# Branch hints ahead of the tests of a mixture-of-experts kernel: three engines are told which way each test goes

## The chip, the cores and the metric

The kernel runs on one core of one Trainium2 chip. The metric is the device time of one execution in microseconds (us). Before the change it was 739.19 us, the median of three runs (738.68 to 739.32). Five engines of the core work side by side, each with a program of its own: TensorE (PE in the profile; PEld is its weight load), VectorE (DVE), ScalarE (ACT), GpSimd (POOL) and SyncE (SP), which here issues the transfers from memory. They wait for each other through semaphores. A letter q behind an engine's name (PEldq, SPq) means its sequencer: waits, branches, register instructions and DMA issues, in which the engine itself stands idle.

## The reference, cut to what matters

Two layers, 256 tokens of width 1024. Each layer is a token mixer (attention, a state-space model and latent attention) and then a mixture of experts, which alone is touched here:

```python
def hier_moe(x, w_rg, b_rg, w_re, b_re, w_gate, w_up, w_down):
    ...                       # gate[n, g, e]: two experts of one group per token, the rest 0
    for g in range(N_EXPERT_GROUPS):           # 4 groups of 8 experts, hidden width 256
        h = jax.nn.silu(jnp.einsum('nd,edf->enf', xt, w_gate[g])) * jnp.einsum('nd,edf->enf', xt, w_up[g])
        h = h * gate[:, g].T[:, :, None].astype(h.dtype)
        y = y + jnp.einsum('enf,efd->nd', h, w_down[g])
```

All 32 experts' weights are read in every layer, 3 MB for each expert. Which tokens go to which expert is known only at run time, and so is the number of tokens that an expert gets.

## The kernel before

The function `moe(l, tab, rt)` takes the experts of a layer in nine blocks, in an order that the table `ORDER` fixes: seven blocks of four experts (here called quads) and two of two experts in layer 0, and the same numbers in layer 1. A block gathers the tokens of its experts by a one-hot matmul (`gather`, L1236), multiplies with the gate and up weights in two halves of the contraction (`gate_up`, L1442), forms the gated hidden values (`hidden`: silu on ACT, L1347, a product on DVE, L1348), transposes them on PE (`hidden_t`), multiplies with the down weights (`down`, L1458), splits the result into a high part (ACT, L1360) and a low part (DVE, L1361), and adds it to the tokens by two more matmuls and an add (`combine`, L1251 to L1253). The add of one block stands behind the gate and up matmuls of the next.

In a quad an expert has 32 places. Should an expert of it have more tokens than that, a second pass over the quad's weights is needed (`second`): the first half of it stands inside a test at L1559 and the other inside a test at L1589, both on the same register `more`, which L1554 loads on every engine. An expert with more than 64 tokens needs extra units: `unit_chain` (L1424) holds seven of them as nested tests, each of which reloads one expert's weights and works 128 places. It stands after the block `UNIT_AT`, the fourth block of layer 0 and the sixth of layer 1, and tests a number `nu` that L1606 loads. With these inputs no unit runs in layer 0 and one runs in layer 1, and one quad in layer 1, the one behind the unit, needs the second pass. All other tests skip their body. A body that is skipped is jumped over on every engine, and in its place an engine runs a few semaphore increments (EVENT_SEMAPHORE at L1424, L1559, L1589), for which others wait.

Weights come through one DMA queue that SP issues (`pump`, L247) in a fixed order into pages of 1 MB, of which there are 25. A page is refilled when the block that read it is done (`done`), and an issue also waits until one of eight earlier transfers has landed. SP goes through the same tests, in its own order. The order of instructions on each engine is the scheduler's of the framework: it moved the test at L1559 behind both halves of `gate_up` in nearly all quads.

## Time and profile before

| what | value |
|---|---|
| median of three runs | 739.19 us |
| the profiled execution | 737.13 us, of which 735.4 us are the span of the program |
| PE busy | 631.6 us, 86% of the span |
| DVE, ACT, POOL busy | 51%, 34%, 15% |
| transfers | 232.90 MB, 317 GB/s over the span |
| first mixture of experts | about 165 to 372 us |
| second mixture of experts | about 505 to 720 us |

The profile cuts the span in 40 slices of 18.4 us. In slices of steady expert work the DMA engines move 400 to 417 GB/s and are busy in nine tenths or more of the time; in the mixers they move far less. The transfers named "instruction" in the profile are the engines' own program code: 53 packets on queue q8 and 34 on queue q14. The 16 KB packets of q8 come as the PE's program goes on, which the prediction uses.

### The profile page before, as it was taken

What the parts mean: (1) busy time and instruction counts of PE and PEld (TensorE: products, weight loads), DVE (VectorE), ACT (ScalarE), POOL (GpSimd) and SP (SyncE); (2) the same over time, 40 slices, a digit from 0 to 9 for tenths busy, and PEclk for the clock granted to TensorE, in tenths of its full rate; (3) what the DMA queues carried; (4) which work ended last, traced back from release to release, by engine and by line L of the source; (5) the groups of instructions that cost most, each with busy time, mean ns of one, the idle gap of its engine ahead of it and who ended that gap; (6) DMA issues with size and microseconds to landing.
All of it is one profiled execution on the core that took longest, in us unless ns stands there. A gap on an engine that the chain in (4) does not pass through costs nothing. (4 is left out here: it accounts for less than half of the span.)

```text
span 735.4 us, 12004 instructions
## 1 busy us (share of the span) xinstructions
PE 631.6 (86%) x4370; PEld 386.3 (53%) x4370; DVE 373.7 (51%) x899; ACT 253.2 (34%) x578; POOL 107.5 (15%) x135
## 2 busy tenths in 40 slices
PE   7997989889799498598799899989899987769994
PEld 6584877744245334336268677775444434324442
DVE  3899977532334117824279878752423324322424
ACT  3647873421012014524074397352111211001113
POOL 1202001000000021521051754510000000000001
PEclk9999999999899799889999999989999999979998
DMA  8920375896999899999994715895999999998992
GB/s 304 419 108 0 117 289 215 331 389 231 413 406 416 280 405 411 412 415 407 398 417 183 286 59 172 302 362 194 333 416 406 392 410 413 416 366 301 410 382 83
DMA packets 57207, 232.90 MB, mean 317 GB/s; under 512 B 6048, under 2 KB 8480, under 8 KB 48160
## 3 DMA queue, kind: packets, MB, share of 16 engines
q1 hardware_dynamic: 57120, 231.75, 81.5%
q8 instruction: 53, 0.87, 0.5%
q14 instruction: 34, 0.28, 0.1%
HBM read 233.82 MB, written 1.05 MB: 319 GB/s over the span
## 5 line engine op out<-in xcount | busy, mean ns | idle before, releaser
L1442 PE MATMUL gu<-pg,xe 128*32 128x512 f32 (+1 forms) x1024 | 147.9, 618 | 12.4 <-DMA pg<-in_w_up_dram 7.1
L1458 PE MATMUL yp<-pg,scr 128*32 128x512 f32 (+2 forms) x560 | 79.4, 639 | 25.9 <-DVEq L1589 11.5
L1442 PEld LDWEIGHTS gu<-pg,xe 128*32 128x32 f32 (+1 forms) x1024 | 48.1, 117 | 96.7 <-issue 91.0
L1236 PE MATMUL gp<-oh,xn 128*128 128x128 f32 (+1 forms) x416 | 71.2, 325 | 4.0 <-DVE oh L1221 2.0
L1236 PEld LDWEIGHTS gp<-oh,xn 128*128 128x128 f32 x416 | 61.4, 197 | 18.6 <-issue 10.6
L1458 PEld LDWEIGHTS yp<-pg,scr 128*32 128x32 f32 (+1 forms) x560 | 22.1, 120 | 73.0 <-issue 58.2
L1361 DVE TENSOR_TENSOR y<-yp,y 128x512 fp32r<-128x512 f32 (+1 forms) x39 | 26.3, 677 | 65.8 <-ACT y L1360 65.8
L1348 DVE SCALAR_TENSOR_TENSOR scr<-gu,gs,scr 128x256 f32<-128x256 f32 x19 | 9.1, 481 | 97.1 <-ACT scr L1347 97.1
L1228 POOL TENSOR_TENSOR pgt<-oh,gate 128x256 f32<-128x256 f32 (+1 forms) x13 | 10.2, 783 | 316.5 <-PE slp L372 304.6
L1253 DVE TENSOR_TENSOR x<-cp,x 128x512 f32<-128x512 f32 x76 | 48.9, 685 | 14.2 <-PE cp L1252 14.2
L1360 ACT CAST y<-yp 128x512 fp32r<-128x512 f32 (+1 forms) x39 | 22.3, 575 | 88.1 <-PE yp L1458 86.6
L359 DVE TENSOR_SCALAR xe<-gp,vec 128x128 f32<-128x128 f32 (+1 forms) x52 | 20.8, 400 | 52.0 <-PE gp L1236 52.0
L355 ACT ACTIVATE xe<-gp,vec 128x128 f32<-128x128 f32 (+1 forms) x52 | 21.3, 409 | 73.3 <-PE gp L1236 73.2
L1347 ACT ACTIVATE scr<-gu 128x256 f32<-128x256 f32 x19 | 7.3, 384 | 102.3 <-PEq L1559 52.3
L1251 PE MATMUL cp<-y,sm 128*128 128x512 f32 x76 | 34.0, 455 | 0.3 <-PEq L1559 0.2
L1252 PE MATMUL cp<-y,sm 128*128 128x512 f32 x76 | 30.4, 409 | 1.5 <-DVE y L1361 1.5
L1058 DVE SCALAR_TENSOR_TENSOR x<-op,rg,x 128x512 f32<-128x512 f32 x24 | 17.9, 749 | 16.8 <-PE op L681 11.9
L1341 ACT ACTIVATE scr<-slp 128x256 f32<-128x256 f32 x20 | 7.8, 388 | 42.2 <-SPq L1424 28.8
L1251 PEld LDWEIGHTS cp<-y,sm 128*128 128x128 f32 x76 | 14.5, 192 | 10.4 <-issue 8.2
L372 PE MATMUL hp<-cst,scr 128*128 128x128 f32 x40 | 9.3, 314 | 12.2 <-DVE scr L1348 11.1
L372 PE MATMUL slp<-cst,pgt 128*128 128x128 f32 x36 | 8.3, 314 | 11.2 <-DVEq L1424 5.9
L1252 PEld LDWEIGHTS cp<-y,sm 128*128 128x128 f32 x76 | 14.3, 193 | 5.5 <-DVE y L1361 3.8
(454 smaller groups left out, 1209.2 us busy)
## 6 DMA issues: line engine op xcount, KB each, us to landing
pg<-in_w_gate_dram SPq DMA_DIRECT2D x128, 512.0 KB, 10.1
pg<-in_w_up_dram SPq DMA_DIRECT2D x128, 512.0 KB, 10.4
pg<-in_w_down_dram SPq DMA_DIRECT2D x56, 1024.0 KB, 11.8
pg<-in_w_o_dram SPq DMA_DIRECT2D x8, 1024.0 KB, 18.0
pg<-in_w_down_dram SPq DMA_DIRECT2D x12, 512.0 KB, 10.4
pg<-in_w_qk_dram SPq DMA_DIRECT2D x4, 1024.0 KB, 14.9
pg<-in_w_nat_dram SPq DMA_DIRECT2D x4, 960.0 KB, 12.8
wgu<-in_w_gate_dram SPq DMA_DIRECT2D x4, 512.0 KB
```

The costliest lines, as they stand in the source:

```text
L355: S.copy(dst, src) if scale is None else S.activation(dst, src, AF.Copy, scale=scale)
L359: e.tensor_scalar(dst, src, scale, None, op0=OP.mult)
L372: PE.transpose(dst, src, ident[:src.shape[0], :src.shape[0]])
L1058: V.scalar_tensor_tensor(xh, p, rg[:, g, tt:tt + 1], xh, op0=OP.mult, op1=OP.add)
L1236: PE.matmul(p[:, :w], xn[:, tt, k, :], P[:, tt].rearrange("p e c -> p (e c)"), start=(tt == 0), stop=(tt == 1))
L1251: PE.matmul(p, Sm[:, 128 * tt:128 * tt + 128], yh[:, c], start=True, stop=False)
L1252: PE.matmul(p, Sm[:, 128 * tt:128 * tt + 128], yl[:, c], start=False, stop=True)
L1253: V.tensor_tensor(x[:, tt, c], p, x[:, tt, c], OP.add)
L1360: S.copy(yh[:, c], yp)
L1361: V.tensor_tensor(yl[:, c], yp, yh[:, c].bitcast(F32), OP.subtract)
L1442: PE.matmul(gu[m * s:m * s + m, :].rearrange("p (a f) -> p a f", a=2), xs(k, s), page(l, "gu", e, hf)[:, :, k % 4, :], start=(k == 0), sto ...
L1458: PE.matmul(yp[m * s:m * s + m, :], hT[:, j, m * s:m * s + m], page(l, "dn", e)[:, j, c], start=(j == 0), stop=(j == 1), tile_position=(0, ...
```

## The change

Ahead of a test, three engines (PE, ACT, DVE) get two instructions: one that forms the condition in a register (REGISTER_ALU) and one that names a coming branch and, by that register, its direction (BRANCH_PREFETCH_HINT). SP and POOL get none. Nothing else is computed, and no semaphore is added. The place of the pair is fixed by `tc.issue_after`: behind the last matmul, activation or vector instruction that the dictionary `at` holds for the engine. The number `nu` is loaded some instructions earlier than before.

```diff
+            at = {}
+            def hint(label, cond):
+                for name, ins in at.items():
+                    with tc.issue_after(ins.ins):
+                        tc.mark_branch_hint_location(label, hint=cond, engines=[getattr(mybir.EngineType, name)])
...
             def hidden(gu, gs):
-                S.activation(sl, gu[:, 0:256], AF.Silu)
-                V.scalar_tensor_tensor(hh, gu[:, 256:512], gs, sl, op0=OP.mult, op1=OP.mult)
+                at["Activation"] = S.activation(sl, gu[:, 0:256], AF.Silu)
+                at["DVE"] = V.scalar_tensor_tensor(hh, gu[:, 256:512], gs, sl, op0=OP.mult, op1=OP.mult)
...
             def unit_chain(nu, u):
-                with tc.If(nu > u):
+                with tc.If(nu > u, label=f"unit{l}_{u}"):
                     if u:
                         unit_load(u)
                     unit(u)
                     if u + 1 < MAXU:
+                        hint(f"unit{l}_{u + 1}", nu > u + 1)
+                    if u + 1 < MAXU:
                         unit_chain(nu, u + 1)
...
+                    if k in (1, 7):
+                        at["PE"] = ins
...
                         if b > 0:
-                            with tc.If(more > 0):
+                            hint(tag + "a", more > 0)
+                            with tc.If(more > 0, label=tag + "a"):
                                 second(blk, w, 0)
...
                     hh = hidden(gu, gs)
+                    if quad:
+                        hint(tag + "b", more > 0)
...
                     if b == UNIT_AT[l]:
+                        n = 2 * MAXU
+                        nu = nc.values_load(uw["ui"][0:1, n:n + 1], min_val=0, max_val=MAXU)
+                        hint(f"unit{l}_0", nu > 0)
                         combine(pend)
                         pend = None
-                        n = 2 * MAXU
-                        unit_chain(nc.values_load(uw["ui"][0:1, n:n + 1], min_val=0, max_val=MAXU), 0)
+                        unit_chain(nu, 0)
```

On PE, at the test of the extra units in layer 0, before: the last of the matmuls of `combine` (cp), the load of `nu` (from the tile ui), the test, and the first matmul of a unit's body (gpu).

```order
L1251 MATMUL cp<-y,sm 128x512
L1252 MATMUL cp<-y,sm 128x512
L1606 TENSOR_LOAD ui
L1424 COMPARE_AND_BRANCH
L1398 MATMUL gpu<-xn,Pu 128x512 x4
```

The same place now, from the last matmul of `down` (yp) on:

```order
L1470 MATMUL yp_2257<-pg,scr 64x512 x4
L1619 TENSOR_LOAD ui
L1336 REGISTER_ALU
L1710 BRANCH_PREFETCH_HINT
L1251 MATMUL cp<-y,sm 128x512
L1252 MATMUL cp<-y,sm 128x512
```

The load and the hint went ahead of the eight matmuls of `combine`, behind which the test (now L1432) follows directly. Inside each of the first six units of the chain stands a pair too, that of the next unit's test:

```order
L1251 MATMUL cp<-y,sm 128x512 x2
L1336 REGISTER_ALU
L1710 BRANCH_PREFETCH_HINT
L1252 MATMUL cp<-y,sm 128x512 x2
L1432 COMPARE_AND_BRANCH
```

There two matmuls stand between the hint and the test.

On PE, at a quad (the third block of layer 0), before: the gate and up matmuls (gu) of both halves, the load of the flag (qi), the test, and the body's first matmuls (gpa).

```order
L372 MATMUL slp<-cst,pgt 128x128 x2
L1442 MATMUL gu<-pg,xe 32x512 x32
L1554 TENSOR_LOAD qi
L1559 COMPARE_AND_BRANCH
L1474 MATMUL gpa<-scr,xn 128x128 x16
```

And now:

```order
L372 MATMUL slp<-cst,pgt 128x128 x2
L1452 MATMUL gu<-pg,xe 32x512 x16
L1566 TENSOR_LOAD qi
L1336 REGISTER_ALU
L1710 BRANCH_PREFETCH_HINT
L1452 MATMUL gu<-pg,xe 32x512 x16
L1336 REGISTER_ALU
L1710 BRANCH_PREFETCH_HINT
L1572 COMPARE_AND_BRANCH
```

The load of the flag and the first pair went into the middle of the matmuls; the second pair, which belongs to the quad's later test, stands directly before the first test. In the whole program PE has 39 such pairs, ACT 40 and DVE 28; those inside units that do not run are jumped over.

## Rows read from the trace of the kernel before

**Rows 1.** Stretches: us, busy time by engine, granted clock, DMA share, GB/s

```profile
262.00:300.00 38.00, 33.79 (x234) 14.88 (x226) 22.71 (x68) 12.78 (x25) 9.06 (x12) 1.00 1.02 414
400.00:505.00 105.00, 96.55 (x602) 73.96 (x602) 74.03 (x190) 57.58 (x137) 45.87 (x52) 0.95 0.65 229
505.00:622.00 117.00, 105.08 (x686) 52.43 (x683) 38.21 (x80) 21.59 (x56) 3.95 (x5) 0.99 0.94 372
664.00:672.00 8.00, 8.00 (x72) 5.08 (x76) 2.89 (x6) 0.75 (x3) 0.00 (x0) 1.00 0.90 263
```

**Rows 2.** What SP's DMA issues waited for, 300 to 385 us: total, times, longest

```profile
SPq L247 <- DMA pg<-in_w_down_dram: 20.7, 15, 2.2
...
SPq L247 <- PEq L1559: 1.3, 1, 1.3
```

**Rows 3.** PE in order of time, 345 to 386 us: start, length, what [idle before]

```profile
357.74 1.91 PE L1442 MATMUL gu<-pg,xe 128*32 128x512 f32 x12 [1.59 <-DMA pg<-in_w_up_dram]
...
368.37 1.90 PE L1458 MATMUL yp<-pg,scr 128*32 128x512 f32 x10 [0.22 <-DMA pg<-in_w_down_dram]
```

**Rows 4.** PE in order of time, 236 to 262 us

```profile
236.74 0.51 PE L1251 MATMUL cp<-y,sm 128*128 128x512 f32 x1
...
238.81 0.39 PE L1252 MATMUL cp<-y,sm 128*128 128x512 f32 x1
244.48 0.66 PE L372 MATMUL slp<-cst,pgt 128*128 128x128 f32 x2 [5.29 <-PEq L1424]
249.48 9.11 PE L1442 MATMUL gu<-pg,xe 128*32 128x512 f32 x64 [4.34 <-issue]
```

**Rows 5.** Line L1424, 200 to 300 us: count, ns min/median/max, first and last start

```profile
L1424 SPq EVENT_SEMAPHORE  x9: 17/17/17, 244.3 to 248.8; - x9
...
L1424 PEldq COMPARE_BRANCH  x1: 5411/5411/5411, 238.7 to 238.7; - x1
```

**Rows 6.** DMA queue q8, 239.5 to 244.2 us: packets, MB, share of 16 engines

```profile
q8 instruction: 1, 0.02, 1.6%
```

**Rows 7.** DMA queue q8, 244.2 to 249.5 us

```profile
q8 instruction: 1, 0.02, 1.1%
```

**Rows 8.** DMA queue q8, 400 to 505 us

```profile
q8 instruction: 4, 0.07, 0.2%
```

**Rows 9.** SP in order of time, 250 to 262 us

```profile
252.85 7.14 SPq L247 DMA_DIRECT2D pg<-in_w_down_dram  x4
```

**Rows 10.** What SP's DMA issues waited for, 236 to 262 us

```profile
SPq L247 <- PEq L1559: 5.0, 1, 5.0
```

**Rows 11.** Stretches of layer 0 behind the test of the units, columns as in rows 1

```profile
252.40:255.30 2.90, 2.90 (x27) 1.99 (x23) 0.00 (x0) 0.00 (x0) 0.00 (x0) 0.84 1.04 410
255.30:258.80 3.50, 3.30 (x32) 1.76 (x24) 0.00 (x0) 0.07 (x1) 0.00 (x0) 1.00 0.98 284
```

**Rows 12.** Line L1424, 600 to 700 us

```profile
L1424 SPq EVENT_SEMAPHORE  x9: 17/17/17, 657.7 to 662.8; - x9
...
L1424 PEldq COMPARE_BRANCH  x3: 70/176/6028, 624.1 to 653.1; - x3
```

**Rows 13.** PE in order of time, 644 to 664.5 us

```profile
654.18 9.71 PE L1442 MATMUL gu<-pg,xe 128*32 128x512 f32 x64
```

**Rows 14.** Waits of all engines, 645 to 672 us

```profile
ACT scr L1341 <- SPq L1424: 17.2, 1, 17.2
DVE scr L1486 <- ACT scr L1341: 9.3, 1, 9.3
```

**Rows 15.** Line L1589, the whole span

```profile
L1589 PEldq COMPARE_BRANCH  x15: 78/318/1681, 182.8 to 717.5; - x15
L1589 ACTq COMPARE_BRANCH  x15: 38/45/50, 183.2 to 717.9; - x15
```

**Rows 16.** Line L1606, the whole span

```profile
L1606 SPq FUSED_REGOPS  x2: 147/156/165, 202.3 to 663.0; - x2
```

**Rows 17.** Line L1554, 655 to 664 us

```profile
L1554 PEldq TENSOR_LOAD <-qi x1: 304/304/304, 661.1 to 661.1; - x1
```

## The prediction

> **What bounds the kernel now.** I read the stretches first, then who the DMA queue waits for, then PE around each test. In the steady part of the experts the DMA engines are busy all the time and move 414 GB/s, while PE is busy in 89% (33.79 of 38 us) [rows 1]. There SP's issues wait for SP's own earlier transfers, 20.7 us of it for down weights alone between 300 and 385 us, and for PE only 1.3 us [rows 2]. PE waits for weights to the end of layer 0: 1.59 us for the last gate and up pages, 0.22 us in the middle of the last down [rows 3]. So the end of an expert stage is set by the moment when its last page lands, and PE time matters only where it holds up an issue of SP or where the queue isn't full: at the start of layer 1's experts (372 GB/s [rows 1]), and at the tests of the extra units.

> The reader should next see the test of the units in layer 0. PE stands idle for 5.29 us, does two small matmuls and stands idle for another 4.34 us, for which the trace finds no waker [rows 4]. The first of the two gaps is PE's branch over all seven units, which takes 5.41 us [rows 5]. In each of the two gaps one 16 KB packet of program code comes on q8 [rows 6, 7]. I take both for fetches of code: the landing place of the jump, and the piece of program behind it. How long a piece is follows from the mixer, which has no branch: 602 matmuls and 602 loads went by with 4 packets [rows 1, 8]. With 4 to 5 fetches in 1204 instructions an estimate is 240 to 300 instructions each. Between the landing and the second gap PE issues the two slp matmuls with their loads, one load of gu, and the waits before them, about ten instructions. The landing thus stands about ten instructions before the end of a piece.

> **The change part by part.**

> 1. *The hint of the units' test on PE, layer 0.* It now stands ahead of eight combine matmuls, and the branch comes behind them. Those matmuls end with the row at 238.81 [rows 4]; eight at about 0.25 us each (the first started at 236.7, the last at 238.8) put the hint some 2 us before the branch. If the fetch starts at the hint and is as long as before, PE goes on 2 us earlier; if the hint is too late to do anything, 0. Both are kept.

> 2. *The moved code on PE, layer 0.* Ahead of the landing PE gets ten pairs: one for the second block, two for the third, one for the units, and six inside the units. These are 20 instructions, and a piece ends at a fixed count. A landing that stood ten before the end of a piece then stands about ten behind it, with some 230 to go. So the second gap, 4.34 us, goes whatever the hint does. This rests on no instruction having been added or taken away elsewhere ahead of it, which the order of PE shows, and on the count of ten, which may be wrong by a few; if it were over 20, the gap would stay.

> 3. *What these are worth.* Without the second gap alone PE starts its 64 gate and up matmuls at about 245.1 and not at 249.48, and is done 9.1 us later, at 254.2 instead of 258.6; with the 2 us of the hint at 252.2. The hidden values need ACT's copy of the places, which waits for SP's last semaphore at 248.8 [rows 5], so ACT is not later than PE. The next work of PE waits for pages. The time is then worth what it gives the DMA queue. SP issued a down page at 252.85 and the next only after a wait of 5.0 us for PE's test at L1559 [rows 9, 10]. For that the queue ran low: 284 GB/s between 255.3 and 258.8, after 410 [rows 11]. The loss is 3.5 us x (1 - 284/410) = 1.1 us. With PE done by 254.2, SP doesn't wait at all and the loss is gone: **-1.1 us**. If only the hint works and the gap stays, PE is done at 256.6 and about 60% of it is gone, -0.65 us. If neither works, 0. Behind it the queue is full up to the end of layer 0 [rows 1, 2], and PE waits for its pages there [rows 3], so these 1.1 us are not lost again; the mixer and layer 1 follow as a chain and shift with them.

> 4. *The units of layer 1.* The jump out after one unit costs PE 6.03 us [rows 12], and the hint stands two matmuls ahead of it, under 1 us. I count nothing: PE did 64 gate and up matmuls until 663.9 [rows 13], and for the second pass behind them it needs DVE (L1486), which waited 9.3 us for ACT, which waited 17.2 us for SP's semaphores at L1424 [rows 14]. SP gives these out from 657.7 to 662.8 [rows 12], each when a transfer of its own has landed, and SP has no hint. An earlier PE would wait for DVE.

> 5. *The quads.* PE's branch takes 318 ns in the middle and 1.68 us at worst [rows 15]; the three slow ones I leave in, since PE's queue or the pages cover them. ACT's branch takes 45 ns [rows 15]: there is nothing to win on ACT, whose first hint stands directly before its test, and little on DVE.

> 6. *The price of the pairs.* Some 28 are run on PE. No row shows one. From below stands a branch of ACT, 45 ns [rows 15], from above SP's register instruction, 156 ns [rows 16], so a pair takes 0.09 to 0.31 us, and 28 of them 2.5 to 8.7 us if all were in the way. I take 0: PE's loads of the flag take 0.30 us and stand in the middle of its matmuls, which ran from 654.18 to 663.9 without an idle row [rows 13, 17], because the sequencer is ahead of the engine. On ACT and DVE the pair follows an instruction behind which the engine waits for PE. Where the cover is gone, at the start of layer 1, the four quads' pairs would add 0.7 to 2.5 us.

> The sum for the profiled execution is 735.4 - 1.1 = 734.3 us of span, and with the 1.73 us around it 736.0 against 737.13. That execution lies 2.06 us below the median, so I carry the difference over: 739.19 - 1.1 = **738.1 us**.

> **The rivals.**

> *Nothing happens* (the hint comes too late, and the landing stays at the end of a piece): 739.2. For it: with quads, too, the pair often stands next to the test. Against it: the 20 added instructions shift the landing without the hint's help.

> *More than the dip is won.* When SP's queue stays full, its later wait for PE of 1.3 us [rows 2] may go as well, and PE is earlier by 6 us, so any such wait in layer 0 shrinks: -1.1 - 1.3 = -2.4, 736.8. Against it: PE then runs on the pages' time again within a block.

> *Slower: a hint takes the place of the code that comes next.* If an engine fetches one piece ahead, and a hint makes it fetch the piece of the branch target in its stead, the engine meets the end of its present piece without the next one. The price is one such gap, 4.34 us [rows 4]. With a full queue a single gap is covered by pages in store; it decides from the first that falls where the queue is not full: among the four quads at the start of layer 1, or in the second pass behind the unit, where PE runs without an idle moment and the queue moves 263 GB/s [rows 1]. One: 739.2 + 4.3 - 1.1 = 742.4; two: 746.7. For it: 13 of 14 quads jump, and pairs of two tests stand together, the later one ahead of the earlier test. Against it: the target of a quad's test lies 140 to 170 instructions on, mostly in the piece that comes next anyway.

> [...]

> **How the numbers follow.** My forecast gets 0.50, nothing 0.18, more 0.17, slower 0.15. A measurement of this kernel tells 0.2%, 1.5 us, from no change. The forecast and "nothing" lie within that; a part of the forecast (0.08) may turn out over 1.5 us, and 0.03 of it slower, by uncovered pairs. So faster is 0.25, the same 0.57, slower 0.18. The range goes from 736.2, a little under the rival that wins more, to 742.3, one uncovered gap; the likeliest case's own range, with the bounds of parts 1, 2 and 6, is 737.0 to 739.9.

> **What would show it.** In layer 0 the profile should show one idle gap of PE of 3 to 5 us at the units' test and none behind the slp matmuls; SP's wait of 5.0 us for PE at L1572 gone; about 410 GB/s in place of 284 right behind; the rest of the trace earlier by about 1 us. In layer 1 ACT should still wait for SP's semaphores until some 661 to 663 us. I am wrong if PE gets new gaps without a waker at quads (slower), if the second gap stays, or if the 1.1 us won at 260 us are not there any more at 372.

## The result, and the profile after

The changed kernel is slower: 762.80 us (median of 4 runs, 757.71 to 765.28) against 739.26 us, a ratio of 1.0292 with a 95% interval of 1.0254 to 1.0329. The forecast was 738.1 us, its range ended at 742.3. The profiled execution took 757.71 us, of which 755.8 us are the span.

PE in order of time, in layer 0, answers to [rows 4] (start, length, what, [idle before <- who ended it]):

```profile
210.62 1.06 PE L1470 MATMUL yp<-pg,scr 128*32 128x512 f32 x7 [1.37 <-DVEq L1604]
216.65 5.39 PE L1470 MATMUL yp<-pg,scr 128*32 128x512 f32 x25 [4.97 <-issue]
...
251.51 0.66 PE L372 MATMUL slp<-cst,pgt 128*128 128x128 f32 x2 [4.97 <-DVEq L1432]
252.10 8.61 PE L1452 MATMUL gu<-pg,xe 128*32 128x512 f32 x64
...
262.85 2.77 PE L1470 MATMUL yp<-pg,scr 128*32 128x512 f32 x23 [0.51 <-ACTq L1604]
268.70 2.60 PE L1470 MATMUL yp<-pg,scr 128*32 128x512 f32 x9 [3.07 <-issue]
```

The second gap of [rows 4], 4.34 us, is gone, as forecast. The first is about as long as before, but now DVE ends it: DVE's own jump over the units, from its branch to its landing, takes 4.8 us (246.6 to 251.4 us) where it took 1.0 us (239.6 to 240.6). New are gaps in the middle of the down matmuls of a quad, for which the trace finds no waker. Over the whole program the page has 13.6 us of such idle time at this line:

```profile
L1470 PE MATMUL yp<-pg,scr 128*32 128x512 f32 (+2 forms) x560 | 84.1, 662 | 39.3 <-issue 13.6
```

In the kernel before, the same group (L1458) is idle for 25.9 us, most of it in waits for DVE, ACT and pages, and none of its gaps over 0.5 us is without a waker. The first new gap has a packet of program code in it (DMA queues, 211.7 to 216.7 us), like the gaps of [rows 6, 7]:

```profile
q8 instruction: 1, 0.02, 1.3%
```

The branch over the units of layer 0, L1432 (count, ns min/median/max, first and last start), which answers to [rows 5]:

```profile
L1432 PEldq COMPARE_BRANCH  x1: 5200/5200/5200, 245.6 to 245.6; - x1
```

And the second instruction of the pairs, L1710:

```profile
L1710 PEldq BRANCH_PREFETCH_HINT  x28: 30/35/40, 179.0 to 731.0; - x28
```

The jump takes 5.20 us where it took 5.41. A hint costs PE 35 ns here, in the middle of 28.

### The profile page after: what moved, and what is told of

Read it like the earlier page. It is cut to its first block, busy times and chain, and to the rows that moved or that the text cites. A ratio compares the mean times of both kernels' runs of the same rounds, so it can differ in the third digit from the quotient of the medians.

```text
span 755.8 us, 12154 instructions
## 1 busy us (share of the span) xinstructions
PE 639.4 (85%) x4370; PEld 391.3 (52%) x4370; DVE 372.9 (49%) x899; ACT 252.6 (33%) x578; POOL 107.1 (14%) x135
## 5 line engine op out<-in xcount | busy, mean ns | idle before, releaser
L1452 PE MATMUL gu<-pg,xe 128*32 128x512 f32 (+1 forms) x1024 | 146.0, 622 | 6.7 <-issue 3.3
L1470 PE MATMUL yp<-pg,scr 128*32 128x512 f32 (+2 forms) x560 | 84.1, 662 | 39.3 <-issue 13.6
L1251 PEld LDWEIGHTS cp<-y,sm 128*128 128x128 f32 x76 | 14.6, 193 | 10.5 <-issue 7.1
L548 PE MATMUL t4p<-ca,tabs 128*32 128x32 f32 (+3 forms) x512 | 16.6, 251 | 3.2 <-issue 3.2
L372 PEld LDWEIGHTS hp<-cst,scr 128*128 128x128 f32 x40 | 6.8, 203 | 23.8 <-DVE scr L1356 11.1
```

What stands on the lines that cost most here:

```text
L548: PE.matmul(t4p[b][32 * jq:32 * jq + 32, c + lo:c + hi], g0[ri][:, 8 * d + i, :], ca[ri][:, 8 * d + i, m, :].rearrange("p m c -> p (m c)") ...
L1251: PE.matmul(p, Sm[:, 128 * tt:128 * tt + 128], yh[:, c], start=True, stop=False)
L1452: ins = PE.matmul(gu[m * s:m * s + m, :].rearrange("p (a f) -> p a f", a=2), xs(k, s), page(l, "gu", e, hf)[:, :, k % 4, :], start=(k == 0 ...
L1470: at["PE"] = PE.matmul(yp[m * s:m * s + m, :], hT[:, j, m * s:m * s + m], page(l, "dn", e)[:, j, c], start=(j == 0), stop=(j == 1), tile_p ...
```

## The experiments

**The same code, with every hint saying "no jump".**

```diff
-  hint(tag + "b", more > 0)
+  hint(tag + "b", more > 0 if (l, b) == (1, 6) else more < 1)     # "a" and the units likewise
```

> The changed kernel with the same instructions in the same places on every engine, but each executed hint now says 'the test will not jump': the register holds the opposite value (for the two tests whose body runs it stays as it was). Nothing of the computation changes. Theory A (an armed hint that says 'jump' takes the place of the fetch of the following piece of PE's program; where test and landing lie in a piece that PE already has, PE meets the end of that piece without the next one): no hint is armed, so the new gaps of PE without a waker are gone (none of 3 to 5 us behind the quads' tests) and the time is 737 to 740 us; the second gap behind the units' test in layer 0 (4.34 us before) stays away, since the code is shifted as in the changed kernel. Theory B (the 107 added pairs of instructions shift the code so that landings fall badly, or cost their own time): same code, same time, 757 to 766 us. Theory C (any hint, whichever way it says, stops the fetch of the following piece): 757 to 766 us as well, with the same gaps.

Measured: 741.94 us, ratio 1.0011 (0.9970 to 1.0052). Same instructions, same places, one bit in a register: the loss is gone. The same stretch of PE as above:

```profile
210.65 3.64 PE L1470 MATMUL yp<-pg,scr 128*32 128x512 f32 x32 [1.47 <-DVEq L1604]
...
244.59 0.66 PE L372 MATMUL slp<-cst,pgt 128*128 128x128 f32 x2 [5.82 <-DVEq L1432]
245.18 8.57 PE L1452 MATMUL gu<-pg,xe 128*32 128x512 f32 x64
```

All 32 down matmuls run without a gap, and the second gap stays away. A packet of program code, which in the changed kernel comes only inside its first new gap, comes here long before, while PE is between the pair of this quad's later test (200.5 us) and that test (206.9 us). DMA queue, 200.5 to 207 us:

```profile
q8 instruction: 1, 0.02, 0.5%
```

In the changed kernel, where pair and test stand at the same times within 0.1 us, no packet comes on q8 in this window: the fetch was not made. B and C fall. No cost of the 28 pairs themselves can be measured (the interval ends at 0.5%).

**Hints on ACT and DVE alone, on the units alone, on the quads alone.**

```diff
-  for name, ins in at.items():
+  for name, ins in [(n, i) for n, i in at.items() if n != "PE"]:               # ACT and DVE
+  for name, ins in at.items() if label.startswith("unit") else ():             # units
+  for name, ins in at.items() if label.startswith("quad") else ():             # quads
```

> Hints on ACT and DVE only, all of them saying which way the test goes; PE's program is that of the kernel before. Theory A: the loss comes from PE's pieces, so PE has the gaps of before and no others (5.3 and 4.3 us at the units' test of layer 0), and the time is 738 to 741 us. Theory B: with PE's code in its old place 738 to 741 us too. Rival D (the pieces of ACT and DVE are displaced as well, and make the hidden values late, which the 8.6 us wait of PE for DVE at 311.65 us in the changed kernel could be): 744 to 755 us.

> Only the hints of the extra units, on all three engines; none at the quads. Theory A: these hints stand in the same piece as their test on PE, too late to change what was fetched on entering it, and no piece ends between hint and test: PE's branch at the units' test stays at 5.0 to 5.6 us, no new gap appears, the second gap of layer 0 goes (the landing is shifted by 14 instructions, past the end of a piece), and the time is 736.5 to 740 us. Theory E (a wrong or late hint makes the jump itself dearer): the branch over the units takes 7 us or more, 742 us or more.

> Only the hints of the quads, on all three engines; none at the units. Theory A: most of the loss is here: 752 to 766 us, with new gaps of PE of 2 to 5 us without a waker, each behind a quad's test and beginning at the end of a piece; the first in the down matmuls of the third block of layer 0 at about 212 us. The landing behind the units is shifted by a few instructions only and stays ahead of the end of a piece, so the second gap there may stay. Theory E: 737 to 741 us, and the units' hints make the loss.

Measured: ACT and DVE 740.69 us, ratio 1.0029 (0.9991 to 1.0066); units 738.18 us, 0.9993 (0.9960 to 1.0026); quads 753.36 us, 1.0202 (1.0140 to 1.0264). So the loss needs PE's hints, those of the quads; D falls. PE's branch over the units of layer 0 took 6.04 us with the units' hints (PE idle for 5.89 us), more than forecast (5.0 to 5.6 us) and less than Theory E asks for (7 us or more), and without a loss of time E falls too. The quads' run has the gap again, behind the seventh matmul:

```profile
208.24 1.06 PE L1470 MATMUL yp<-pg,scr 128*32 128x512 f32 x7 [1.37 <-DVEq L1604]
214.44 5.14 PE L1470 MATMUL yp<-pg,scr 128*32 128x512 f32 x25 [5.14 <-issue]
```

Units and quads together lose more (2.9%) than the quads alone (2.0%). The changed kernel has four gaps without a waker in the down matmuls, 13.6 us, the quads' run three, 10.8 us, in part at other places. By Theory A that can be, since the units' pairs shift the code behind them and with it which hints are in force when a piece ends; that this is the reason is not shown.

**Quad hints directly before their test.**

```diff
-  hint(tag + "a", more > 0)                  # ahead of the first test
-  hint(tag + "b", more > 0)                  # behind hidden()
...
+  at["PE"] = at.get("cp") or at["PE"]        # the add's last matmul
+  hint(tag + "b", more > 0)
   with tc.If(more > 0, label=tag + "b"):
```

> The changed kernel with its hints of the quads' later tests moved on PE to directly before the test (behind the last matmul of the add), true direction as in the changed kernel; the hints of the quads' first tests are left out, those of the units stay. Theory A (loss only where a piece of PE's program ends between hint and test, or between the entry of a piece and the test): in all quads but one hint and test are neighbours, so no piece ends between them: no new gaps of PE but at most one (4.7 us, in the down matmuls of the quad behind the units of layer 0, where the hint still stands ahead of the first test); 738 to 744 us. Theory F (a true hint that says 'jump' costs a fetch wherever it stands): 750 to 763 us.

Measured: 743.47 us, ratio 1.0061 (1.0029 to 1.0092). Of the new gaps in down matmuls one is left, and it is the one that was named:

```profile
263.95 1.91 PE L1470 MATMUL yp<-pg,scr 128*32 128x512 f32 x2 [3.53 <-issue]
```

So the place of the later tests' hints decides, not that there are any: F falls. The first tests' hints are left out in this run, so it doesn't tell what those cost. The time is still 0.6% over the kernel before, clear of zero; the one gap is a part of that, the rest was not traced.

**One hint that says "jump", all others "no jump".** The edit is against e1_never:

```diff
-  ... if (l, b) == (1, 6) else more < 1)
+  ... if (l, b) in ((0, 2), (1, 6)) else more < 1)
```

> All hints say 'no jump' as in the run e1_never, but for a single one that executes with its true direction 'jump': that of the later test of the third block of layer 0 (on all three engines). Theory A: PE enters a piece with this hint armed, and that piece holds both the test and its landing; so one new gap of 4.5 to 5.5 us in the down matmuls of that quad, behind the seventh of them, at about 210 to 217 us; no other new gap. The price by itself is the gap less what the queue has in store: 1 to 5 us over e1_never (741.9 us), 743 to 747 us. Theory F or a cost that only many hints together have: no gap there, 742 us.

Measured: 741.58 us, ratio 1.0043 (0.9992 to 1.0093). The gap stands where it was forecast, and it is the only new one in the down matmuls:

```profile
212.35 1.06 PE L1470 MATMUL yp<-pg,scr 128*32 128x512 f32 x7 [1.37 <-DVEq L1604]
218.44 5.32 PE L1470 MATMUL yp<-pg,scr 128*32 128x512 f32 x25 [5.02 <-issue]
...
242.20 3.65 PE L1470 MATMUL yp<-pg,scr 128*64 128x512 f32 x16
```

The time rises by less than forecast: the runs don't resolve it from that of e1_never. PE comes to the next block's down matmuls 29.85 us after the first row (242.20 - 212.35), in e1_never 22.07 us (232.72 - 210.65), so the gap of 5.02 us made PE 7.8 us late. This is a stretch with a full queue (405 GB/s in the gap, 405 and then 422 behind it), and by the end of the layer most of it is won back (the last block's down matmuls start at 369.48 us, in e1_never at 366.15, and e6_one was 1.7 us later from the start).

**The hint one piece earlier.**

```diff
-  for name, ins in at.items():
+  for name, ins in (at or AT).items() if label.startswith("unit") else ():
...
+  if (l, b) in ((0, 2), (1, 5)):             # a block's add, one piece ahead of the units' test
+      nu = nc.values_load(uw["ui"][0:1, n:n + 1], min_val=0, max_val=MAXU)
+      hint(f"unit{l}_{l}", nu > l, {"PE": at["cp"]})
...
-  if u + 1 < MAXU:
+  if u + 1 < MAXU and (l, u) != (1, 0):      # layer 1: the second test beside the first
       unit_chain(nu, u + 1)
```

> No hints at the quads. The hint of the units' test that jumps stands on PE one piece of program earlier: in layer 0 behind the add of the third block, in layer 1 behind the add of the sixth (for that the test of the second unit in layer 1 stands beside the first test, not inside it). ACT and DVE keep the units' hints of the changed kernel. Theory A (the hint decides what is fetched when the next piece is entered): PE enters the piece with the test while the hint is armed and fetches the landing instead of the following piece, so the jump takes under 1 us in both layers, against 5 to 6 us before, without a second gap behind it. The time gains little, since ACT and DVE wait for SP's semaphores in both layers: 735 to 740 us. Theory G (PE can't fetch a landing ahead of the jump at all): the branch stays at 5 to 6 us.

> As e7_early, and SP too gets a hint ahead of the units' test of each layer (59 and 20 instructions of SP ahead of it). In the kernel before SP's jump in layer 1 took 5.2 us (652.4 to 657.7 us), and PE, DVE and ACT wait behind its semaphores until 662.8 us. If SP's hint is in time by Theory A, SP's jump takes under 1 us, its semaphores are out 4 to 5 us earlier, and with PE's early jump layer 1 gains 3 to 5 us: 732 to 737 us. If the hint is in the same piece as the test, nothing changes against e7_early: 735 to 740 us.

Measured: 734.04 us, ratio 0.9936 (0.9902 to 0.9969); with SP's hint 733.16 us, 0.9931 (0.9899 to 0.9963). SP's hint moved nothing: its semaphores at L1432 come from 659.5 to 664.7 us there and from 658.0 to 663.6 us without it. Its time lies in the range that was forecast for a hint of SP that works, but e7_early comes as low without one. PE's branches over the units in e7_early (L1432), in layer 0 and then in layer 1:

```profile
L1432 PEldq COMPARE_BRANCH  x1: 345/345/345, 240.1 to 240.1; - x1
```

```profile
L1432 PEldq COMPARE_BRANCH  x3: 78/191/357, 625.0 to 648.4; - x3
```

5.2 and 6.1 us in the changed kernel have become 0.35 us, and G falls. In layer 0 this gives nothing, since DVE's jump is still long there (its branch at 240.7 us, its landing at 246.4 us). PE's first matmul behind the units of layer 0:

```profile
246.53 0.66 PE L372 MATMUL slp<-cst,pgt 128*128 128x128 f32 x2 [5.88 <-DVEq L1432]
```

Three more runs, timed against each other on one chip, ask what of this is the hint (edits against e7_early; the third run is e7_early itself):

```diff
-  hint(f"unit{l}_{l}", nu > l, {"PE": at["cp"]})
+  hint(f"unit{l}_{l}", nu < l + 1, {"PE": at["cp"]})                            # e9_split
-  for name, ins in (at or AT).items() if label.startswith("unit") else ():
+  for name, ins in (at or AT).items() if at and "cp" not in at and list(at) == ["PE"] else ():   # e10_two
```

> The kernel of e7_early with the same instructions, but PE's two early hints say 'no jump'. It tells what of the gain of e7_early (0.64%) comes from the hints on PE and what from the test of layer 1 that stands beside the first one, from the shifted code and from the hints on ACT and DVE. Theory A: PE's jumps take 5 to 6 us again in both layers, and the time is that of the kernel before, 738 to 741 us. Theory H (the gain comes from the new place of the test): 733 to 736 us with long jumps.

> The kernel of e7_early with only its two early hints on PE; no other hint on any engine, so the code behind the units' test of layer 0 is shifted by 2 instructions and not by 14. Theory A: both jumps take under 1 us; in layer 0 the landing stands some 5 instructions ahead of the end of a piece again, so the second gap (4.3 us in the kernel before) comes back behind the first two small matmuls. The gain of layer 1 stays; that of layer 0 shrinks by up to 1 us: 733.5 to 737 us. Theory I (the gain hangs on the hints of ACT and DVE): 738 to 741 us.

> e7_early once more, on the chip of e9_split and e10_two, to compare the three directly: 732 to 736 us, 0.4 to 1.0% under the kernel before.

Measured: e9_split 739.70 us, ratio 1.0003 (0.9980 to 1.0026); e10_two 739.54 us, 0.9989 (0.9964 to 1.0013); e11_early_again 734.59 us, 0.9920 (0.9891 to 0.9948). With the bit turned PE's jumps are long again, 5.39 us in layer 0, and 6.26 us in layer 1, the longest of its three branches at L1432 there:

```profile
L1432 PEldq COMPARE_BRANCH  x3: 70/173/6255, 626.2 to 652.7; - x3
```

and the gain is gone. So the gain needs PE's hints, and H falls. The packets agree with Theory A: between 236 and 252 us, around the jump of layer 0, two packets of program code come on q8 in e9_split and one in e7_early, in which PE had the landing already. So a hint that says "jump" does not merely stop a fetch. PE's hints by themselves are not enough: e10_two, which was forecast at 733.5 to 737 us, has short jumps of PE too (0.35 and 0.37 us), but there DVE's own jump in layer 1 takes 6.6 us, and PE waits for it. PE's first matmul behind the units of layer 1, in e10_two and then in e11_early_again:

```profile
657.34 0.66 PE L372 MATMUL slp<-cst,pgt 128*128 128x128 f32 x2 [7.01 <-DVEq L1432]
```

```profile
647.40 0.41 PE L372 MATMUL slp<-cst,pgt 128*128 128x128 f32 x2 [1.30 <-DVEq L1432]
```

In e11_early_again DVE's code holds the units' pairs, and its jump is short. The hint that DVE runs there says "no jump", and in e1_never DVE's jump is short as well (0.9 us, in the kernel before 5.6), so it is the shifted code and not the hint that helps DVE: Theory I had the time of e10_two right, and not the reason. In layer 0, by the same reading, the shift made DVE's jump long (235.7 to 241.4 us in e11_early_again). There e10_two, without pairs on DVE, has both jumps short, PE goes on after 1.56 us of idle time, and the whole still shows no gain; no run has both jumps short in both layers. The version of e7_early and e11_early_again beats both kernels, the one before by 0.6 to 0.8%.

## Why the prediction was wrong, point by point

**The step that failed.** The forecast put the quads' hints at nothing (part 5), and they alone cost 2.0% (753.36 us). The slower rival had what became Theory A, "a hint takes the place of the code that comes next", and 0.15. It was put low by the sentence against it: the target of a quad's test lies "mostly in the piece that comes next anyway". That is the case that does the harm. By Theory A a hint in force when PE enters the next piece names that piece itself, which PE is already in, and the fetch that would have brought the one behind it is not made: in the third block of layer 0 the packet of 200.5 to 207 us is missing, and PE stands idle for 4.97 us. The sentence looked at where the landing lies seen from the hint, and not at where PE is when it next chooses what to fetch. The order of the instructions showed what was needed: the pair of a quad's later test stands ahead of its earlier test, and in most quads the gather and the add of a block lie between that pair and its own test, and in the third block, by Theory A, a piece ends there.

**The price.** One gap was put at 4.34 us, and one or two of them were counted. The profile has four in the down matmuls (4.97, 3.07, 3.65 and 1.91 us) and two at gate and up matmuls (2.08 and 1.18 us); e1_never has none of the six. The two gaps that were followed cost PE more than their idle time. That of 5.02 us in e6_one made PE 7.8 us late. The 31 us around the gap of 3.65 us in layer 1 (columns as in [rows 1]):

```profile
540.86:571.83 30.97, 25.68 (x110) 12.43 (x110) 6.93 (x15) 4.08 (x10) 1.05 (x1) 0.78 1.00 389
```

And the same work in e1_never:

```profile
533.14:555.53 22.39, 20.75 (x110) 11.48 (x110) 6.93 (x15) 4.08 (x10) 1.05 (x1) 1.00 1.02 413
```

In the gap and for 4 us behind it the granted clock was 0.50; over the next 5.8 us (551.2 to 557 us) it was 0.62 in the mean, and behind that 1.00. In e1_never, without this gap, it is 1.00. The 110 matmuls of these two rows took 25.68 us in place of 20.75. The stretch is 8.6 us longer (30.97 - 22.39): 3.7 us idle and 4.9 us at the lower clock. Not all of that is the gap's: the 16 matmuls ahead of it already ran at 0.71 in the mean and took 2.61 us, where all 32 take 3.64 us in e1_never.

In layer 1 this comes out at the end, since there SP waits for PE. The longest of the waits of SP's issues in the changed kernel, 505 to 640 us:

```profile
SPq L247 <- PE yp L1470: 26.3, 3, 10.0
```

This row is 3.4 us in e1_never and 15.2 us in the kernel before, where other rows of PE stand in its place; all that SP's issues wait for PE in this stretch is 53 us in the changed kernel, 23 us in e1_never and 30 us before. The forecast said that PE's time matters only where it holds up an issue of SP; this fits, and there PE was held up. Between the profiled executions of e1_never and of the changed kernel, 742.12 and 757.71 us, PE's down matmuls of the last block of layer 0 (366.15, 375.32 us) are 9.2 us apart, the last ones of the program 15.6 us (728.99, 744.56 us).

**Part 1, the units' hint on PE in layer 0.** Its two ends were 2 us and 0; it is next to 0 (5.20 us after 5.41). By Theory A the hint stood in the same piece as its test, and what was to be fetched had been chosen on entering it. The part also left out DVE, whose jump became long here (4.8 us after 1.0), so that a short one of PE could have won nothing. What a hint in time is worth to PE's jump, e7_early and e9_split show: 0.35 us with the earlier hint saying "jump", when PE had the landing ready, and 5.39 us with the same hint saying "no jump".

**Part 2, the second gap.** It went, in the changed kernel and in all eleven runs, so the number came out right, but perhaps by luck. The reason given, a landing ten instructions ahead of the end of a piece and 20 added ones, is not shown: the trace has 53 packets of code on q8 with 0.87 MB, 16 KB each, and that a piece so ends at a fixed count of instructions was the author's estimate; and the gap went too in e2_act_dve, where PE has the matmuls and branches of before, and in e10_two, where 2 instructions were added and it was expected back. The trace has the same seven semaphore instructions of PE around this place in both, all ahead of the first gate and up matmul in e2_act_dve, four ahead of the gap and three behind it in the kernel before. Why the gap went stays open.

**Part 3, its worth.** The 1.1 us can't be seen: e3_units, without the second gap and without a wait of SP for PE in this place, has 0.9993 (0.9960 to 1.0026), and from 234 to 276 us its queue moves 349 GB/s, in the kernel before 351. In the changed kernel SP's wait for PE's test at L1572, which should have gone, is still 3.7 us.

**Parts 4 to 6.** In layer 1 ACT did wait for SP's semaphores, which came until 677.5 us here. But "an earlier PE would wait for DVE" was wrong. In e11_early_again the first matmuls of the second pass (gpa) start at 656.45 us, right behind the gate and up matmuls, and SP's semaphores come until 658.8 us; an early PE with an early DVE is worth 5 us (e11_early_again against e9_split, where PE is late in layer 1, and against e10_two, where DVE is), where the forecast counted nothing. The quads' branch of PE, left out as covered, reached 4.45 us at L1572 (365.1 to 369.6 us), with one packet of code on q8 inside it. The price of the pairs was rightly put at nothing; a pair takes PE 72 ns (37 and 35), under the lower bound of 0.09 us.

## What to carry to other kernels

By Theory A a hint that says "jump" changes the one fetch that PE makes when it enters its next piece of code; its forecasts of gaps and jumps came true here, but for the second gap in layer 0. The hint made PE's jump short where it stood, by the estimate of a piece, one piece ahead of the branch (0.35 us in e7_early, 5.39 us with the bit turned in e9_split), and the time fell where no other engine's jump held PE up at the landing (0.9920 in e11_early_again; 0.9989 in e10_two, where DVE's jump in layer 1 takes 6.6 us). Where test and landing both lie, by Theory A, in the piece that PE enters next, a packet was missing and PE stood idle for 4.97 us; turn the hint's register over to see in one run what it costs (741.94 us in e1_never against 762.80). A jump can become long or short with added instructions and no hint that says "jump": DVE's over the units of layer 0 took 1.0 us in the kernel before and 5.6 us in e1_never (238.8 to 244.4 us). Count an idle gap of PE with the slow clock behind it: in e6_one the granted clock was 0.75 in the gap and 0.61 in the 5.6 us behind it, and 5.02 us of idle made PE 7.8 us late.

## What the runs showed of the hardware

Without an early hint PE's jump over the units took 4.2 us (e4_quads, layer 0, with PE idle for 4.09 us) to 6.3 us (e9_split, layer 1), with one 0.35 us (e7_early). PE stood idle without a waker in the middle of matmuls of one kind, too. In the changed kernel 128 matmuls of the next layer's tables took 5.08 us, with a gap of 2.10 us ahead of them and one of 1.12 us behind:

```profile
350.20 5.08 PE L548 MATMUL t4p<-ca,tabs 128*32 128x96 f32 x128 [2.10 <-issue]
```

Gaps of 1.80 and 1.07 us stand at these matmuls and behind them in e1_never, and one of 1.58 us in the kernel before, so the hints did not make them. In the changed kernel one packet of code comes on q8 from 347.5 to 350.2 us, at the first of its two gaps, and one while the 128 matmuls run (350.2 to 355.3 us). A reading, not tested: 128 matmuls and their 128 loads are about a piece by the prediction's estimate, and PE waits there for code.
